# A two-layer hybrid encoder trunk: later key and query transposes, the last channel sum on VectorE, and two output blocks in one feature loop

## The chip, the cores and the metric

The kernel runs on one core of one Trainium2 chip. The metric is the time of one execution on the device in microseconds. The kernel before was run three times: 2420.48, 2420.87 and 2423.06 us, a median of 2420.87. One further execution was taken with the hardware profiler, and every row below is of that one.

## The reference

Two inputs, a prompt of 256 tokens and a sample of 512, go through the same two layers. They share weights and nothing else. Cut to what is computed:

```python
for l in range(2):
    h = rms_norm(x, g_mix[l])
    q, k, v, u, gl = split(h @ w_in[l])
    q, k = rope(rms_norm(q per head)), rope(rms_norm(k per head))
    a = attention(q, k, v)              # 8 heads, 2 key heads, head size 128
    z = u[:1024] * sigmoid(u[1024:])
    z = depthwise_conv(z, 31 taps)      # each channel by itself
    c = silu(layer_norm(z)) @ w_pw[l]
    ga, gc = split(sigmoid(gl + b_gate[l]))
    x = x + (ga * a + gc * c) @ w_out[l]
    h2 = rms_norm(x, g_ffn[l])
    gate, up = split(h2 @ w_gu[l])
    x = x + (silu(gate) * up) @ w_down[l]
return rms_norm(x, g_final)
```

All is float32 with 1024 features, so eight blocks of 128 features.

## The kernel before

**Layout.** Features lie on the 128 partitions and the 768 tokens of both inputs along the rows. A float32 operand of TensorE is split into a high and a low fp32r part (`hi`/`lo`, `Thi`/`Tlo`), and every product is made in three passes: high by high, low by high, high by low (`PASSES`, `proj_a` and `proj_two` from L485 on). Eight PSUM banks are handed out in turn (`PS`, L192), so a new tile waits until the one eight tiles earlier has been read.

**The order.** The program is emitted by one planner. `Clock` (L54) keeps TensorE's time so far: `mm` (L202) and `turn` (L206) add the estimated cost of a matmul and of a transpose. Work that depends on other engines is put down with `clock.at(dt, job)` or `clock.later(dt, job)` and emitted when the planner's clock has passed the due time; `later` also lets a job be called sooner, once. Between these, `tap` (L764) fills VectorE with the taps of the depthwise convolution: 31 instructions for each of eight blocks in each layer, on 783 columns. The engines run their queues in the order in which the instructions were emitted.

**Keys and queries.** `rope_body` projects each of six token tiles (`q0p`, `kp`), and `rotate` (L673) turns the pair of heads: ScalarE copies out of PSUM and squares, VectorE multiplies out of PSUM into `q0r` or `kr`, GpSimd does the two remaining products into `q0t` and the addition. For k, `scale_k` (L700) multiplies on ScalarE after a GpSimd rsqrt (L218). `flip` (L706) then transposes both halves on TensorE (`kT`, `q0T`), and ScalarE and VectorE split the result. The flips come due at `K_FLIP` and `Q_FLIP` (used at L731 to L734) after the last projection, and at the latest with the first score that needs them. After q come the gate projections (`gl_0`, `gl_1`) and the convolution's inputs (`ua`, `ug`).

**Scores.** `h0t0s` is the score tile of head 0 and token tile 0; its sum, reciprocal (`h0t0st`) and scale (`h0t0p`) go over VectorE and ScalarE before TensorE transposes it (`h0t0T`).

**Channel norm.** When a block's 31 taps are done, `add` (L775) adds it into `ysum` on GpSimd. After the eighth, `channel_norm` (L1410) comes due: TensorE takes the mean with a matrix of ones (`mean`), VectorE subtracts it from each block (`centre`, L1423), ScalarE squares (`square`, L1424), VectorE adds the squares (`add`, L1430), and TensorE takes the variance (`var`). A sum comes due 1.0 after its square was put down.

**Output.** Attention and the convolution branch are mixed into eight feature blocks, each split by ScalarE (`mThi`) and VectorE (`mTlo`). `out_body` (L993) multiplies by the output weights: eight output blocks, each in two halves of 384 tokens, each half 24 matmuls (eight features, three passes) and an addition into `x` by VectorE. The loop at L1014 makes blocks 0 to 3 one step each and blocks 4 to 7 a step together.

Of the kernel before, what the change touches and what calls it, by code (L numbers as in the profile page):

```python
# [17 lines left out]
ALU = mybir.AluOpType  # L18
# [137 lines left out]
def trunk(tc, x_in, x_tok, w_a, w_qkv, w_pw, w_out, w_gu, w_down, vecs, gqk, rope, y_out):  # L156
# [4 lines left out]
    with ExitStack() as ctx:  # L161
# [333 lines left out]
            yield  # L495
            return ps

        def proj_two(ws, hT, s, names):

            t0, n = SPLITS[s]  # L500
            ps = [PS(name) for name in names]
            for k in range(KC):
                for w, o in zip(ws, ps):
                    for p, (a, b) in enumerate(PASSES):
                        mm(o[:, :n], w[a][:, k * P:(k + 1) * P], hT.cols(k, b, s),
                           k == 0 and p == 0, k == KC - 1 and p == 2)
# [122 lines left out]
        def layer_blocks(l):  # L629
# [127 lines left out]
            def conv(j, z):  # L757
                wcol = lambda k: vcol(l, V_WDW, k * KC + j)

                def first():  # L760
                    y.y[j] = UC(nm(f"y{j}"))
                    vector.tensor_scalar(y.y[j], z[:, :CONV_N], wcol(0), vcol(l, V_BDW, j), op0=ALU.mult, op1=ALU.add)

                def tap(k):  # L764
                    def f():
                        vector.scalar_tensor_tensor(y.y[j], z[:, k:k + CONV_N], wcol(k), y.y[j],
                                                    op0=ALU.mult, op1=ALU.add)
                    return f

                def last():  # L770
                    y.z_live -= 1
                    tap(CK - 1)()
                    clock.at(1.5, add)

                def add():  # L775
                    if y.ysum is None:
                        y.ysum = XP(nm("ysum"))[:, :CONV_N]
                        nc.gpsimd.tensor_copy(y.ysum, y.y[j])
                    else:
                        nc.gpsimd.tensor_tensor(y.ysum, y.ysum, y.y[j], op=ALU.add)  # L780
                    y.convs += 1
                    if y.convs == KC:
                        clock.at(LN_AFTER, lambda: channel_norm(y))

                taps = [tap(k) for k in range(1, CK - 1)] + [last]
                clock.waiting.append([first] + taps)
# [206 lines left out]
            def out_body(*js):  # L993
                def body(ws):
                    if js[0] == 0:
                        for f in y.gates:
                            f()
                        for j in range(KC):
                            y.xs.append(X(nm(f"x{j}"), j))
                            nc.sync.dma_start(y.xs[j], x_in[j] if l == 0 else x_dram[j])  # L1000
                        y.norm2 = ffn_norm()
                    for s, (t0, n) in enumerate(HALVES):
                        for e, j in enumerate(js):
                            ps = yield from proj_a(ws[e], y.mT, s, nm(f"o{j}_{s}"), HALVES)
                            xs = y.xs[j][:, t0:t0 + n]
                            vector.tensor_tensor(xs, ps[:, :n], xs, op=ALU.add)
                            y.norm2.add(j, s)
                            if s == 1:
                                ws.free(e)
                            if (s, j) == (1, KC - 2):  # L1010
                                weights.next = clock.now + SUMS_AT
                return body

            for js in tuple((j,) for j in range(KH)) + (tuple(range(KH, KC)),):  # L1014
                stream.add([(l, f"out:{j}") for j in js], nm(f"wo{js[0]}"), [w_out[l, j] for j in js], out_body(*js))


# [392 lines left out]
        def channel_norm(y):  # L1410
            l, nm, ys = y.l, y.nm, y.y
            chain = clock.chains[2]
            mean, rstd, sqs = [], [], []
            y.normed = Once(lambda: None)

            def means():
# [5 lines left out]

            def centre(j):  # L1423
                def square():  # L1424
                    sq = Z(nm(f"sq{j}"))
                    act(sq[:, :CONV_N], ys[j], AF.Square)
                    sqs.append(sq)
                    clock.at(1.0, add)

                def add():  # L1430
                    if j:
                        a, b = sqs[0][:, :CONV_N], sqs.pop()[:, :CONV_N]
                        vector.tensor_tensor(a, a, b, op=ALU.add)
# [207 lines left out]
SIG_FIRST = 0.3  # L1641
SIG_EACH = 0.65
K_SCALE = 5.0
K_FLIP = 11.6
Q_FLIP = 10.0
LO_POOL = ((1,), (1, 3))
ADD_POOL = (1, 3, 5)
N_ACC = 0.8
# [80 lines left out]
```

## Time and profile before

| | |
|---|---|
| median of three runs | 2420.87 us (2420.48 to 2423.06) |
| the profiled execution | 2419.15 us |
| its span | 2417.4 us |
| mean granted TensorE clock | 0.972 of full speed |
| DVE busy | 1930.8 us (80%) |
| ACT busy | 1135.9 us (47%) |
| POOL busy | 1300.8 us (54%) |

The span is the time from the first instruction to the last; what lies around it is 1.75 us. PE is TensorE's matmuls and transposes, PEld its weight loads, DVE VectorE, ACT ScalarE, POOL GpSimd. A row of the timeline reads: start, duration, engine, line, operation, output<-input, shape, count, and in brackets the idle time of the engine before it with the instruction that ended it. Tile names have lost their numbers: `L_q0r` is q0r of any layer. An instruction's duration can overlap the next one's start on the same engine.

### The profile page before, as it was taken

To read this page: it belongs to the slowest core of one execution; us is meant where nothing else is said; L and a number is where in the kernel's file an instruction comes from. 1 tells how busy PE (TensorE), PEld (TensorE's weight loads), DVE (VectorE), ACT (ScalarE), POOL (GpSimd) and SP (SyncE) were. 2 spreads that over 40 slices of the span, in tenths; PEclk is the share of its full clock that TensorE was granted. 3 is DMA by queue.
4 is the path that set the end of the run, shared out by engine and by line. 5 is a ranking of instruction groups with operands and counts; after the bars stand their busy time and mean duration, and the time that the engine had idled before them with its cause. 6 is when DMAs were issued, how large, how long until landed. Compare 5 with 4: busy or idle time off the path is not lost. (4 is left out here: it accounts for less than half of the span.)

```text
span 2417.4 us, 34958 instructions
## 1 busy us (share of the span) xinstructions
PE 2239.3 (93%) x13276; PEld 2102.1 (87%) x13276; DVE 1930.8 (80%) x2478; ACT 1135.9 (47%) x2281; POOL 1300.8 (54%) x958
## 2 busy tenths in 40 slices
PE   8898999999979999999998899999999799999997
PEld 7778888888979999999987787888889699999997
DVE  5899999755287798797978999996553877887888
ACT  5324554684244444444443255556833444444443
POOL 4943553532266666666668444535322766666664
PEclk9899999999989999999998999999999899999999
DMA  4111111133212343343421111212341134334332
GB/s 166 36 61 64 58 49 60 64 106 135 97 53 97 126 144 110 128 147 109 157 81 51 53 47 59 66 63 73 112 159 53 35 122 140 122 123 140 122 123 88
DMA packets 72425, 229.60 MB, mean 95 GB/s; under 512 B 8128, under 2 KB 15296, under 8 KB 72256
## 3 DMA queue, kind: packets, MB, share of 16 engines
q1 hardware_dynamic: 72256, 227.37, 27.4%
q8 instruction: 104, 1.70, 0.3%
q14 instruction: 65, 0.53, 0.1%
HBM read 208.46 MB, written 18.87 MB: 94 GB/s over the span
## 5 line engine op out<-in xcount | busy, mean ns | idle before, releaser
L133 DVE SCALAR_TENSOR_TENSOR L_y<-L_z,vec,L_y 128x783 f32<-128x783 f32 x480 | 625.9, 1338 | 2.5
L214 POOL TENSOR_TENSOR wq_L_wgu_0m<-T_L_wgu,wq_L_wgu_0m 128x512 fp32r<-128x512 f32 x168 | 228.4, 1375 | 173.4 <-ACT wq_L_wgu_0m L211 173.4
L211 ACT ACTIVATE wq_L_wgu_0m<-T_L_wgu 128x512 fp32r<-128x512 f32 x168 | 102.6, 630 | 258.5 <-DVE T_L_wgu L133 209.3
L214 POOL TENSOR_TENSOR wq_L_wgu_0m<-st_L_wgu,wq_L_wgu_0m 128x512 fp32r<-128x512 f32 x126 | 179.5, 1426 | 43.3 <-ACT wq_L_wgu_0m L211 43.3
L214 POOL TENSOR_TENSOR lo_L_wgl<-st_L_wgl,hi_L_wgl 128x1024 fp32r<-128x1024 f32 x32 | 101.5, 3178 | 147.9 <-ACT hi_L_wgl L211 121.1
L203 PE MATMUL L_gl<-L_h1h,hi_L_wgl 128*128 128x512 f32 (+1 forms) x512 | 177.7, 347 | 0.6 <-DVE L_h1t4m L133 0.6
L203 PE MATMUL L_gl<-L_h1h,lo_L_wgl 128*128 128x512 f32 (+1 forms) x512 | 174.4, 341 | 0.0
L203 PE MATMUL L_gl<-L_h1l,hi_L_wgl 128*128 128x512 f32 (+1 forms) x512 | 174.0, 340 | 0.0
L214 POOL TENSOR_TENSOR lo_L_wqkv<-st_L_wqkv,hi_L_wqkv 128x1024 fp32r<-128x1024 f32 x24 | 65.4, 2724 | 129.1 <-ACT hi_L_wqkv L211 118.2
L214 POOL TENSOR_TENSOR lo_L_wu<-st_L_wu,hi_L_wu 128x1024 fp32r<-128x1024 f32 (+1 forms) x32 | 82.9, 2594 | 50.4 <-ACT hi_L_wu L211 50.4
L214 POOL TENSOR_TENSOR lo_L_wo<-st_L_wo,hi_L_wo 128x1024 fp32r<-128x1024 f32 x16 | 39.5, 2468 | 127.2 <-ACT hi_L_wo L211 127.2
L203 PEld LDWEIGHTS L_gl<-L_h1h,lo_L_wgl 128*128 128x128 f32 x512 | 97.6, 191 | 11.2
L203 PEld LDWEIGHTS L_gl<-L_h1h,hi_L_wgl 128*128 128x128 f32 x512 | 97.9, 191 | 10.3 <-DVE L_h1t4m L133 0.9
L203 PEld LDWEIGHTS L_gl<-L_h1l,hi_L_wgl 128*128 128x128 f32 x512 | 97.9, 191 | 9.7
L203 PE MATMUL L_o<-L_mThi,hi_L_wo 128*128 128x384 f32 x256 | 88.5, 346 | 6.8 <-ACT L_mThi L211 6.8
L214 POOL TENSOR_TENSOR lo_L_wpw<-st_L_wpw,hi_L_wpw 128x1024 fp32r<-128x1024 f32 x16 | 40.0, 2503 | 100.0 <-ACT hi_L_wpw L211 95.2
L133 DVE TENSOR_TENSOR L_dl<-L_silu,L_dh 128x384 fp32r<-128x384 f32 x80 | 59.5, 782 | 41.1 <-ACT L_dh L211 41.1
L203 PE MATMUL L_c<-L_zsh,hi_L_wpw 128*128 128x256 f32 (+1 forms) x256 | 90.2, 352 | 0.0
L203 PE MATMUL L_ua<-L_h1h,hi_L_wu 128*128 128x256 f32 (+1 forms) x256 | 90.0, 352 | 0.0
L203 PE MATMUL L_ug<-L_h1h,lo_L_wu 128*128 128x256 f32 (+1 forms) x256 | 87.4, 342 | 2.7 <-DVE lo_L_wu L133 2.7
L211 ACT ACTIVATE wq_L_wgu_0m<-st_L_wgu 128x512 fp32r<-128x512 f32 x126 | 78.5, 623 | 22.8 <-POOL wq_L_wgu_0m L214 19.4
L203 PE MATMUL L_ua<-L_h1h,lo_L_wu 128*128 128x256 f32 (+1 forms) x256 | 89.0, 348 | 0.1
(1629 smaller groups left out, 7918.6 us busy)
## 6 DMA issues: line engine op xcount, KB each, us to landing
st_L_wgu<-w_gu SPq DMA_DIRECT2D x88, 512.0 KB, 3.5
st_L_wu<-w_a SPq DMA_DIRECT2D x32, 512.0 KB, 3.5
st_L_wgl<-w_a SPq DMA_DIRECT2D x32, 512.0 KB, 3.5
st_L_wqkv<-w_qkv SPq DMA_DIRECT2D x24, 512.0 KB, 3.5
st_L_wpw<-w_pw SPq DMA_DIRECT2D x16, 512.0 KB, 3.7
st_L_wo<-w_out SPq DMA_DIRECT2D x16, 512.0 KB, 3.7
g_dram<-L_sgl SPq DMA_DIRECT2D x16, 384.0 KB, 2.4
L_gj<-g_dram SPq DMA_DIRECT2D x16, 384.0 KB, 4.3
```

Source lines behind the costliest of these rows:

```text
L133: return f(out, *args, **kw)
L203: nc.tensor.matmul(out, lhsT, rhs, start=start, stop=stop)
L211: nc.scalar.activation(out, in_, func, **kw)
L214: engine.tensor_tensor(lo, x, hi.bitcast(F32), op=ALU.subtract)
```

## The change

`K_FLIP` goes from 11.6 to 21.0 and `Q_FLIP` from 10.0 to 13.0. The eighth addition into `ysum` is issued on VectorE instead of GpSimd. The sums of squares keep their due times, but when a square is put down, sums are issued early until at most one is left waiting. Output blocks 0 and 1 become one step; their first halves go through `proj_two`, which gets a parameter for the token halves, and their second halves follow one after the other.

```diff
--- before.py
+++ after.py
@@ -495,9 +495,9 @@
             yield
             return ps
 
-        def proj_two(ws, hT, s, names):
-
-            t0, n = SPLITS[s]
+        def proj_two(ws, hT, s, names, parts=SPLITS):
+
+            t0, n = parts[s]
             ps = [PS(name) for name in names]
             for k in range(KC):
                 for w, o in zip(ws, ps):
@@ -777,7 +777,8 @@
                         y.ysum = XP(nm("ysum"))[:, :CONV_N]
                         nc.gpsimd.tensor_copy(y.ysum, y.y[j])
                     else:
-                        nc.gpsimd.tensor_tensor(y.ysum, y.ysum, y.y[j], op=ALU.add)
+                        engine = vector if y.convs == KC - 1 else nc.gpsimd
+                        engine.tensor_tensor(y.ysum, y.ysum, y.y[j], op=ALU.add)
                     y.convs += 1
                     if y.convs == KC:
                         clock.at(LN_AFTER, lambda: channel_norm(y))
@@ -1000,8 +1001,11 @@
                             nc.sync.dma_start(y.xs[j], x_in[j] if l == 0 else x_dram[j])
                         y.norm2 = ffn_norm()
                     for s, (t0, n) in enumerate(HALVES):
+                        two = None
+                        if js[0] == 0 and s == 0:
+                            two = yield from proj_two([ws[e] for e in range(2)], y.mT, s, [nm(f"o{j}_{s}") for j in js], HALVES)
                         for e, j in enumerate(js):
-                            ps = yield from proj_a(ws[e], y.mT, s, nm(f"o{j}_{s}"), HALVES)
+                            ps = two[e] if two else (yield from proj_a(ws[e], y.mT, s, nm(f"o{j}_{s}"), HALVES))
                             xs = y.xs[j][:, t0:t0 + n]
                             vector.tensor_tensor(xs, ps[:, :n], xs, op=ALU.add)
                             y.norm2.add(j, s)
@@ -1011,7 +1015,7 @@
                                 weights.next = clock.now + SUMS_AT
                 return body
 
-            for js in tuple((j,) for j in range(KH)) + (tuple(range(KH, KC)),):
+            for js in ((0, 1), (2,), (3,), tuple(range(KH, KC))):
                 stream.add([(l, f"out:{j}") for j in js], nm(f"wo{js[0]}"), [w_out[l, j] for j in js], out_body(*js))
 
 
@@ -1410,7 +1414,7 @@
         def channel_norm(y):
             l, nm, ys = y.l, y.nm, y.y
             chain = clock.chains[2]
-            mean, rstd, sqs = [], [], []
+            mean, rstd, sqs, adds = [], [], [], []
             y.normed = Once(lambda: None)
 
             def means():
@@ -1422,10 +1426,12 @@
 
             def centre(j):
                 def square():
+                    while len(adds) > 1:
+                        adds.pop(0)()
                     sq = Z(nm(f"sq{j}"))
                     act(sq[:, :CONV_N], ys[j], AF.Square)
                     sqs.append(sq)
-                    clock.at(1.0, add)
+                    adds.append(clock.later(1.0, add))
 
                 def add():
                     if j:
@@ -1641,8 +1647,8 @@
 SIG_FIRST = 0.3
 SIG_EACH = 0.65
 K_SCALE = 5.0
-K_FLIP = 11.6
-Q_FLIP = 10.0
+K_FLIP = 21.0
+Q_FLIP = 13.0
 LO_POOL = ((1,), (1, 3))
 ADD_POOL = (1, 3, 5)
 N_ACC = 0.8
```

TensorE, first layer, before: the last projections of q0 around the key transposes; `kT0` and `kT1` are the two key heads, in two banks each.

```order
L203 MATMUL L0_q0p4_969<-hi_L0_wqkv2_1_625,L0_h1l1_351 128x256
L203 MATMUL L0_q0p4_969<-lo_L0_wqkv2_1_626,L0_h1h1_350 128x256
L207 MATMUL L0_kT0_0_999<-ident_137,L0_kr0_569 128x128 x3
L207 MATMUL L0_kT0_1_1003<-ident_137,L0_kr1_570 128x128 x3
L207 MATMUL L0_kT1_0_1013<-ident_137,L0_kr0_569 128x128 x3
L207 MATMUL L0_kT1_1_1017<-ident_137,L0_kr1_570 128x128 x3
L203 MATMUL L0_q0p5_1031<-hi_L0_wqkv2_0_563,L0_h1h1_350 128x256
L203 MATMUL L0_q0p5_1031<-hi_L0_wqkv2_0_563,L0_h1l1_351 128x256
```

After: the same transposes stand between gate matmuls.

```order
L203 MATMUL L0_gl0_1_1081<-L0_h1l1_351,hi_L0_wgl0_0_795 128x512
L203 MATMUL L0_gl0_1_1081<-L0_h1h1_350,lo_L0_wgl0_0_796 128x512
L207 MATMUL L0_kT0_0_1110<-ident_137,L0_kr0_569 128x128 x3
L207 MATMUL L0_kT0_1_1114<-ident_137,L0_kr1_570 128x128 x3
L207 MATMUL L0_kT1_0_1124<-ident_137,L0_kr0_569 128x128 x3
L207 MATMUL L0_kT1_1_1128<-ident_137,L0_kr1_570 128x128 x3
L203 MATMUL L0_gl0_1_1081<-L0_h1h1_350,hi_L0_wgl0_0_795 128x512
L203 MATMUL L0_gl0_1_1081<-L0_h1l1_351,hi_L0_wgl0_0_795 128x512
```

The remaining q0 projections, `gl0_0` and the first 18 matmuls of `gl0_1` have come ahead of the twelve transposes.

TensorE, first layer, before: the channel mean, between two groups of the last q projection `q3p5`.

```order
L203 MATMUL L0_q3p5_4312<-hi_L0_wqkv5_0_3763,L0_h1l1_351 128x256
L203 MATMUL L0_q3p5_4312<-lo_L0_wqkv5_0_3764,L0_h1h1_350 128x256
L203 MATMUL L0_mean0_4329<-L0_ysum_1286,ones_142 128x256
L203 MATMUL L0_mean1_4331<-L0_ysum_1286,ones_142 128x512
L203 MATMUL L0_h4t5s_4335<-L0_kThi1_1011,L0_q2Thi0_3481 128x512
L203 MATMUL L0_h4t5s_4335<-L0_kThi1_1011,L0_q2Tlo0_3482 128x512
L203 MATMUL L0_h4t5s_4335<-L0_kTlo1_1012,L0_q2Thi0_3481 128x512
L203 MATMUL L0_q3p5_4312<-hi_L0_wqkv5_1_3867,L0_h1h1_350 128x256
```

After: the channel mean inside a gate projection.

```order
L203 MATMUL L0_gl5_0_4359<-L0_h1h0_183,hi_L0_wgl5_0_3958 128x256
L203 MATMUL L0_gl5_0_4359<-L0_h1l0_184,hi_L0_wgl5_0_3958 128x256
L203 MATMUL L0_gl5_0_4359<-L0_h1h0_183,lo_L0_wgl5_0_3959 128x256
L203 MATMUL L0_mean0_4377<-L0_ysum_1312,ones_142 128x256
L203 MATMUL L0_mean1_4379<-L0_ysum_1312,ones_142 128x512
L203 MATMUL L0_gl5_0_4359<-L0_h1h0_183,hi_L0_wgl5_0_3958 128x256
L203 MATMUL L0_gl5_0_4359<-L0_h1l0_184,hi_L0_wgl5_0_3958 128x256
```

The score matmuls `h4t5s`, the end of `q3p5` and half of `gl5_0` now stand before the mean instead of behind it.

VectorE, first layer, before: from the last taps of block `y7` to the first subtraction of the mean.

```order
L133 TENSOR_TENSOR L0_h4t2pTlo_4163<-L0_h4t2T_4164,L0_h4t2pThi_4162 128x4x128
L133 SCALAR_TENSOR_TENSOR L0_y7_3708<-L0_z7_3353,vec_114,L0_y7_3708 128x783 x2
L133 TENSOR_REDUCE L0_h4t4st_4213<-L0_h4t4s_4209 128x1
L133 TENSOR_TENSOR L0_q3r0_4071<-L0_q3p2_4178,L0_tab0_445 128x256
L133 TENSOR_TENSOR L0_h4t0m_4224<-L0_h4t0av_4217,L0_sgl4_3871 128x256
L133 TENSOR_TENSOR L0_q3r1_4072<-L0_q3p3_4231,L0_tab0_445 128x256
L133 RECIPROCAL L0_h4t4st_4213<-L0_h4t4st_4213 128x1
L133 TENSOR_TENSOR L0_q3r1_4072<-L0_q3p4_4270,L0_tab0_445 128x256
L133 TENSOR_TENSOR L0_h4t2pTlo_4163<-L0_h4t3T_4286,L0_h4t2pThi_4162 128x4x128
L133 TENSOR_TENSOR L0_y0_504<-L0_y0_504,L0_mean0_4329 128x256
```

After: the same stretch of VectorE.

```order
L133 TENSOR_TENSOR L0_q3r0_4070<-L0_q3p2_4177,L0_tab0_445 128x256
L133 TENSOR_TENSOR L0_h4t0m_4223<-L0_h4t0av_4216,L0_sgl4_3869 128x256
L133 SCALAR_TENSOR_TENSOR L0_y7_3675<-L0_z7_3352,vec_114,L0_y7_3675 128x783
L133 TENSOR_TENSOR L0_q3r1_4071<-L0_q3p3_4230,L0_tab0_445 128x256
L133 RECIPROCAL L0_h4t4st_4212<-L0_h4t4st_4212 128x1
L133 TENSOR_TENSOR L0_ysum_1312<-L0_ysum_1312,L0_y7_3675 128x783
L133 TENSOR_TENSOR L0_q3r1_4071<-L0_q3p4_4269,L0_tab0_445 128x256
L133 TENSOR_TENSOR L0_h4t2pTlo_4162<-L0_h4t3T_4285,L0_h4t2pThi_4161 128x4x128
L133 TENSOR_REDUCE L0_h4t5st_4333<-L0_h4t5s_4329 128x1
```

The addition into `ysum` stands three rows behind the block's last tap; the first subtraction of the mean comes later, behind the reduction of `h4t5s`.

TensorE, first layer, before: the start of the output projection; `o0_0` is block 0, first half.

```order
L203 MATMUL L0_o0_0_5889<-L0_mThi0_5112,hi_L0_wo0_0_5557 128x384
L203 MATMUL L0_o0_0_5889<-L0_mTlo0_5113,hi_L0_wo0_0_5557 128x384
L203 MATMUL L0_o0_0_5889<-L0_mThi0_5112,lo_L0_wo0_0_5558 128x384
L203 MATMUL L0_o0_0_5889<-L0_mThi1_5202,hi_L0_wo0_0_5557 128x384
L203 MATMUL L0_o0_0_5889<-L0_mTlo1_5203,hi_L0_wo0_0_5557 128x384
L203 MATMUL L0_o0_0_5889<-L0_mThi1_5202,lo_L0_wo0_0_5558 128x384
L203 MATMUL L0_o0_0_5889<-L0_mThi2_5332,hi_L0_wo0_0_5557 128x384
```

After: `o1_0` is block 1, first half.

```order
L203 MATMUL L0_o0_0_5889<-L0_mThi0_5112,hi_L0_wo0_0_5557 128x384
L203 MATMUL L0_o0_0_5889<-L0_mTlo0_5113,hi_L0_wo0_0_5557 128x384
L203 MATMUL L0_o0_0_5889<-L0_mThi0_5112,lo_L0_wo0_0_5558 128x384
L203 MATMUL L0_o1_0_5890<-L0_mThi0_5112,hi_L0_wo0_1_5672 128x384
L203 MATMUL L0_o1_0_5890<-L0_mTlo0_5113,hi_L0_wo0_1_5672 128x384
L203 MATMUL L0_o1_0_5890<-L0_mThi0_5112,lo_L0_wo0_1_5673 128x384
L203 MATMUL L0_o0_0_5889<-L0_mThi1_5202,hi_L0_wo0_0_5557 128x384
L203 MATMUL L0_o0_0_5889<-L0_mTlo1_5203,hi_L0_wo0_0_5557 128x384
L203 MATMUL L0_o0_0_5889<-L0_mThi1_5202,lo_L0_wo0_0_5558 128x384
L203 MATMUL L0_o1_0_5890<-L0_mThi1_5202,hi_L0_wo0_1_5672 128x384
```

Each feature is now used for both blocks before the next one is.

## Rows read from the trace of the kernel before

**Rows 1.** Page, busy time of each engine in the whole span.

```profile
PE 2239.3 (93%) x13276; PEld 2102.1 (87%) x13276; DVE 1930.8 (80%) x2478; ACT 1135.9 (47%) x2281; POOL 1300.8 (54%) x958
```

**Rows 2.** TensorE's waits: what waited, releaser, us in total, times, longest.

```profile
PE L_kT L207 <- ACT L_kr L211: 16.0, 6, 7.7
...
PE L_mean L203 <- POOL L_ysum L780: 10.0, 2, 5.1
...
PE L_o L203 <- ACT L_mThi L211: 6.8, 2, 3.5
```

**Rows 3.** Windows: stretch, length, busy time by engine, PEclk, DMA share, GB/s.

```profile
88.89:99.13 10.24, 5.76 (x22) 4.44 (x23) 3.05 (x5) 6.78 (x28) 9.88 (x10) 0.50 0.15 51
96.08:445.62 349.54, 321.38 (x2039) 289.25 (x2038) 339.26 (x377) 169.49 (x374) 175.59 (x122) 0.97 0.18 59
447.29:454.12 6.83, 4.85 (x11) 3.36 (x12) 3.72 (x9) 4.51 (x16) 5.04 (x8) 0.50 0.06 19
1645.37:1648.78 3.41, 3.41 (x7) 2.01 (x8) 2.06 (x5) 1.05 (x5) 2.90 (x6) 0.50 0.00 0
```

**Rows 4.** Timeline of TensorE at the key transposes and the first score transpose.

```profile
92.62 0.47 PE L207 MATMUL L_kT<-ident,L_kr 128*128 128x128 f32 x1 [7.71 <-ACT L_kr L211]
...
182.71 0.69 PE L207 MATMUL L_h0t0T<-ident,L_h0t0p 128*128 128x128 f32 x2 [6.32 <-ACT L_h0t0p L211]
```

**Rows 5.** Timeline of ScalarE: the scaling of k and of the first score.

```profile
92.16 3.62 ACT L211 ACTIVATE L_kr<-L_kr,L_kr 128x128 f32<-128x128 f32 x12 [16.31 <-POOL L_kr L218]
...
182.15 0.51 ACT L211 ACTIVATE L_h0t0p<-L_h0t0p,L_h0t0st 128x256 f32<-128x256 f32 x1 [0.37 <-DVE L_h0t0st L133]
```

**Rows 6.** Timeline of VectorE at the output blocks of both layers.

```profile
610.77 0.69 DVE L133 TENSOR_TENSOR L_mTlo<-L_mj,L_mThi 128x512 fp32r<-128x512 f32 x1 [0.70 <-ACT L_mThi L211]
...
621.93 0.56 DVE L133 TENSOR_TENSOR L_x<-L_o,L_x 128x384 f32<-128x384 f32 x1 [3.64 <-PE L_o L203]
...
626.13 0.56 DVE L133 TENSOR_TENSOR L_x<-L_o,L_x 128x384 f32<-128x384 f32 x1 [3.64 <-PE L_o L203]
...
1822.84 0.56 DVE L133 TENSOR_TENSOR L_x<-L_o,L_x 128x384 f32<-128x384 f32 x1 [3.66 <-PE L_o L203]
```

**Rows 7.** Timeline of VectorE at the q0 projections.

```profile
96.08 0.42 DVE L133 TENSOR_TENSOR L_q0r<-L_q0p,L_tab 128x256 f32<-128x256 f32 x1 [7.72 <-ACT L_q0t L211]
...
101.10 0.41 DVE L133 TENSOR_TENSOR L_q0r<-L_q0p,L_tab 128x256 f32<-128x256 f32 x1
```

**Rows 8.** Timeline of GpSimd behind the q0 projections.

```profile
107.80 3.14 POOL L214 TENSOR_TENSOR lo_L_wu<-st_L_wu,hi_L_wu 128x1024 fp32r<-128x1024 f32 x1
...
113.31 1.33 POOL L694 TENSOR_TENSOR L_q0r<-L_q0r,L_q0t 128x256 f32<-128x256 f32 x1
```

**Rows 9.** Timeline of GpSimd: the last channel sum, first layer.

```profile
447.38 1.84 POOL L780 TENSOR_TENSOR L_ysum<-L_ysum,L_y 128x783 f32<-128x783 f32 x1
```

**Rows 10.** Timeline of TensorE: the channel mean, first layer.

```profile
449.27 2.93 PE L203 MATMUL L_mean<-L_ysum,ones 128*128 128x256 f32 x4 [4.87 <-POOL L_ysum L780]
```

**Rows 11.** Timeline of VectorE ahead of the channel mean.

```profile
443.03 2.60 DVE L133 SCALAR_TENSOR_TENSOR L_y<-L_z,vec,L_y 128x783 f32<-128x783 f32 x2
445.55 0.68 DVE L133 TENSOR_REDUCE L_h4t4st<-L_h4t4s 128x1 f32<-128x512 f32 x1
```

**Rows 12.** Tile view of sq: durations in ns, min/median/max, first and last start.

```profile
L133 DVE TENSOR_TENSOR L_sq<-L_sq,L_sq x14: 965/976/3046, 458.3 to 1673.6; 128x783 f32<-128x783 f32 x14
```

**Rows 13.** Timeline of TensorE: the first output matmul of each layer.

```profile
603.64 0.33 PE L203 MATMUL L_o<-L_mThi,hi_L_wo 128*128 128x384 f32 x1
...
1798.97 0.34 PE L203 MATMUL L_o<-L_mThi,hi_L_wo 128*128 128x384 f32 x1
```

**Rows 14.** Timeline of GpSimd: the weight split of output block 1.

```profile
583.61 2.41 POOL L214 TENSOR_TENSOR lo_L_wo<-st_L_wo,hi_L_wo 128x1024 fp32r<-128x1024 f32 x1 [8.95 <-ACT hi_L_wo L211]
```

**Rows 15.** Page, costliest groups: count, busy us, mean ns of one, idle before.

```profile
L133 DVE SCALAR_TENSOR_TENSOR L_y<-L_z,vec,L_y 128x783 f32<-128x783 f32 x480 | 625.9, 1338 | 2.5
```

**Rows 16.** Tile view of y: the same taps, min/median/max in ns.

```profile
L133 DVE SCALAR_TENSOR_TENSOR L_y<-L_z,vec,L_y x480: 1003/1027/3181, 49.3 to 1640.2; 128x783 f32<-128x783 f32 x160
```

## The prediction, made before the changed kernel was run

> **What bounds the kernel now.** I read the busy times first, then TensorE's waits by what released them, then the stretches around each edited place, and last the single rows there. TensorE (PE) is busy 2239.3 of the span's 2417.4 us [rows 1], so a gain has to come from its idle time or from time that it spends at half clock. The waits that the edits touch are those of the key transposes (kT: 16.0 us in 6 waits, the longest 7.7), of the channel norm's mean (10.0 us in 2) and of the first output block (o: 6.8 us in 2) [rows 2]. The long ones of kT and of the mean are followed by a stretch in which the granted clock is 0.50, the lower of TensorE's two levels, against 0.97 over the long stretch behind it [rows 3]. A wait thus costs its own length and then half of what TensorE does in that stretch.
>
> Not every such microsecond is worth one. From 96.08 to 445.62 us VectorE (DVE) is busy 339.26 of 349.54 us and TensorE 321.38 [rows 3]: there VectorE paces the stage, and what TensorE gains before it is lost where it next waits for VectorE. At the mean and at the output blocks TensorE paces what follows.
>
> **Key and query transposes (K_FLIP, Q_FLIP).** Before, TensorE stops at 84.91 and starts the transposes at 92.62, released by ScalarE's scaling of k, which itself waited 16.31 us for GpSimd's rsqrt [rows 4, 5]. After, 24 matmuls of 256 columns for q, 24 for gl_0 and 18 of 512 for gl_1 stand ahead of them. At 0.175 us for one of 384 columns (24 output matmuls lie between the sums at 621.93 and 626.13: 4.20 us [rows 6]), in proportion 0.117 for 256 and 0.233 for 512, they fill 2.8 + 2.8 + 4.2 = 9.8 us: TensorE comes to the transposes at 94.7, when ScalarE's twelve scalings, from 92.16 to 95.78 [rows 5], are nearly done. The old wait goes. But the q groups moved ahead take PSUM banks in turn, and the transposes then need the banks that VectorE's four q0r products must read first. These come one by one, the first at 96.08 + 0.42, the last at 101.10 + 0.41 = 101.5 [rows 7]: VectorE waits 7.72 us for a ScalarE copy behind those same scalings, which the edit does not move, and has two taps between any two products. From 94.7 to 101.5 are 6.8 us; with the transposes in between I count 5.7 us of new waits against the 7.7 removed. With the half clock that may go (5.76 us busy at 0.50, so 2.9 [rows 3]) TensorE is 5 to 6 us ahead there. GpSimd follows with a weight split of 3.14 us at 107.80 and the last q0r at 113.31 [rows 8], for which the query transposes wait; Q_FLIP moves these too, and about 2 us are left at the next weights. All of it ends at the first score transposes: they wait 6.32 us for a ScalarE scale at 182.15 that VectorE's sum releases [rows 4, 5], and the same taps stand ahead of that sum on VectorE. So I take **0** for both layers, with 0 to +6 us a layer as bounds (a loss would need bank waits beyond 7.7 + 2.9, and the banks give at most 6.8): the cover is that wait of 6.32 us, and if VectorE were faster there the gain would show.
>
> **The last channel sum on VectorE, the order of the square sums.** Before, TensorE waits 4.87 us at the mean until 449.27, that is from 444.40, for a GpSimd addition of 1.84 us at 447.38, behind GpSimd's rope work [rows 9, 10]. After, three score matmuls of 512 columns, 12 of q3p and 12 of gl_0 of 256 come ahead of the mean: 0.7 + 1.4 + 1.4 = 3.5 us, so TensorE arrives at 447.9. VectorE does, from 443.03, two taps (2.60), a reduction (0.68) [rows 11], three products near 0.42 and a reciprocal, which with overlaps of about 0.08 ends at 447.3; then the addition. It waits for nothing but GpSimd's seventh addition, a block earlier, so nothing behind it on VectorE is held up by more than its own length. The trace has none of this kind on VectorE; the nearest is the square sum, two inputs of 128x783 from SBUF: 965 ns at the shortest, 976 in the middle, 3046 at the longest [rows 12]. From 0.97 to 3.05, I take 1.5, since nothing of GpSimd's is certain to stand beside it. The mean is ready at 448.8 and TensorE waits 0.9 us (0.3 to 2.4). Gain: 4.87 of wait, 2.42 of half clock (4.85 busy at 0.50 [rows 3]), less 0.9, is 6.4 us. In the second layer the wait is 5.1 [rows 2], the half-clock stretch holds 3.41 us [rows 3], so 5.1 + 1.7 - 0.9 = 5.9. Sum 12.3. From it go 1.7, an even chance in each layer that the short new wait still ends in a half-clock stretch of 3.4 us, and 1.0 for the variance behind it: its eight squares (ScalarE) and seven sums (VectorE) end by my schedule when TensorE arrives, 0 to 2 us late, 0.5 a layer. The `adds` list adds no instruction: still seven sums, the first behind four subtractions of the mean instead of three, so that its square is further on when VectorE comes to it. That leaves **9.6 us**.
>
> The Trainium skill ("SBUF — State Buffer", section "SBUF: two separate sides") says that VectorE and GpSimd share a port pair as an exclusive lock, taken for a whole instruction by a VectorE operation with two SBUF inputs against a GpSimd operation that reads SBUF. The spread from 965 to 3046 ns of the square sums agrees with that [rows 12]. By it the new addition costs 0.97 or about 3, never the 1.5 that I took: with a free port in both layers my forecast would be 2398.6, with a locked one 2402.8.
>
> **Two output blocks in one feature loop.** Before, the first output block begins at 603.64 [rows 13], and 21 of its 24 matmuls (7 features, 3.7 us) are done by 607.3; the eighth feature's high part comes just before 610.77 and its low part 0.69 later [rows 6]: the wait of 3.3 us, 3.5 in the other layer [rows 2]. After, the second block's first half stands beside it, 42 matmuls or 7.35 us for seven features: TensorE reaches the eighth at 611.0 and waits about 0.35 for the low part at 611.46. Its weights are split by 583.61 + 2.41 = 586.0 [rows 14], ahead of their earlier use. Both blocks are 96 matmuls, 16.8 us, in either order. Before, the fourth sum into x begins at 626.13; after, at 603.64 + 16.8 + 0.1 + 0.35 = 620.9, so 5.2 us. (Of the 22.5 us before, matmuls and wait explain 20.1; the rest I put down to half clock behind the wait, as at the mean.) Second layer: 1822.84 [rows 6] against 1798.97 [rows 13] + 16.8 + 0.1 + 0.5 = 1816.4, so 6.4. Sum **11.6 us**, from 9 (the low part 1.3 us later in both layers) to 12.6 (no wait at all). The first sum into x comes 0.1 us earlier or later, and blocks 2 to 7 are bound by TensorE: nothing waits for what moved.
>
> **Sum.** 0 + 9.6 + 11.6 = 21.2 us. The profiled execution took 2419.15 us, 1.75 over its span, and becomes 2398.0; it lies 1.7 below the median of 2420.87, from which the change gives 2399.7. I predict **2400 us**, own range 2394 to 2405 (new addition free or locked, transposes a little above 0).
>
> **Rivals.**
> - *The mean's gain is given back in the channel norm.* The mean comes earlier, but VectorE's work between it and the variance does not shrink: seven sums at 0.98 are 6.8 us, and three of them that become 3.05 [rows 12] take 6.2 us, which is the gain of a layer. For it: GpSimd's moved rope work now falls beside them. Against: ScalarE's and VectorE's shares in that stretch are 4.51 and 3.72 of 6.83 us [rows 3], so they have room. Only the output term stays: 2420.87 - 11.6 = 2409.
> - *TensorE paces the first stage after all.* Then kT's 16.0 [rows 2] counts as well: 2399.7 - 16.0 = 2384. For it: TensorE is busy 321 of 349 us there. Against: VectorE 339, and the new bank waits.
> - *The waits come back under other names* and the change does not do what it says: TensorE stops as long at the banks, at the variance, at the last feature. 2421, no change. Against: at the output blocks both times follow from counts of matmuls alone.
> - *Slower: VectorE's taps are held up more by GpSimd.* The 480 taps take 1338 ns in the mean [rows 15] and 1027 in the middle [rows 16], 149 us over. Moving the q and k work changes which GpSimd instruction lies beside which tap through the whole stage that VectorE paces. A quarter more is 37 us, less 21: 2437. It decides from 21 us on, which is 44 ns more a tap. Against: the same GpSimd instructions are there, only in another place.
>
> The lock named above from the Trainium skill ("SBUF — State Buffer", "SBUF: two separate sides") is what would make that last rival; taps at 1003 and at 3181 ns agree with it [rows 16], and no row tells how many meet in the new order.
>
> **How the numbers follow.** Forecast 0.58; given back in the channel norm 0.18; first stage paced by TensorE 0.08; no change 0.09; slower 0.07. Within 0.2% (2416 to 2425.7, about what a measurement of this kernel can tell from no change) is the fourth alone; faster is 0.58 + 0.18 + 0.08 = 0.84; slower 0.07. The range runs from 2386, close to the second rival, to 2412, which takes in the first rival; about 0.2 is left out.
>
> **What would show it.** At the mean, a TensorE wait of 0.3 to 2.4 us released by VectorE, and a ysum addition on VectorE of 1 to 3 us. At the output blocks, a wait under 1 us and the fourth sum into x 17.3 us after the first matmul. kT waits released by VectorE's q0r instead of ScalarE, and a longer wait at the first score transposes, by as much as TensorE is ahead: if that wait keeps its 6.3 us while it starts earlier, VectorE was not the pace and I am wrong by up to 16 us. A mean tap above 1.38 us would make me wrong on the other side.

## The result and the profile after

The changed kernel took 2403.61 us (2401.79 to 2405.50, four runs) against 2421.97 us of the kernel before, measured with it: a ratio of 0.9933, 95% interval 0.9921 to 0.9944. Measured again beside the later experiments it gave 0.9936 (0.9924 to 0.9949). So it is 13.6 to 19 us faster. 2400 was forecast, with a range from 2386 to 2412.

TensorE's waits in the kernel after, in the columns of [rows 2]:

```profile
PE L_h0t0T L207 <- ACT L_h0t0p L211: 19.8, 2, 10.7
PE L_h3t3T L207 <- ACT L_h3t3p L211: 11.1, 2, 5.5
PE L_kT L207 <- DVE L_q0r L133: 10.5, 6, 2.0
PE L_h1t3T L207 <- ACT L_h1t3p L211: 6.4, 2, 3.2
...
PE L_mean L203 <- DVE L_ysum L133: 3.2, 2, 1.6
...
PE L_o L203 <- DVE L_mTlo L133: 0.6, 2, 0.3
```

The three waits of [rows 2] have shrunk or changed their releaser: kT waits for VectorE's q0r, the mean for VectorE's sum, the output only for the last low part. In their place stand longer waits for score scales (h0t0T, h3t3T, h1t3T). Of these, the kernel before had the first two, and none at h1t3T:

```profile
PE L_h0t0T L207 <- ACT L_h0t0p L211: 12.5, 2, 6.3
...
PE L_h3t3T L207 <- ACT L_h3t3p L211: 4.5, 2, 2.3
```

To see what is left of the gain one has to compare places. TensorE in the kernel after, at the key transposes, at the first scores of head 0 and head 4, at the mean, and at a late score of head 5; first layer, then second:

```profile
96.36 0.33 PE L207 MATMUL L_kT<-ident,L_kr 128*128 128x128 f32 x1 [1.47 <-DVE L_q0r L133]
...
98.78 0.33 PE L207 MATMUL L_kT<-ident,L_kr 128*128 128x128 f32 x1 [1.87 <-DVE L_q0r L133]
...
101.33 0.47 PE L207 MATMUL L_kT<-ident,L_kr 128*128 128x128 f32 x1 [2.01 <-DVE L_q0r L133]
...
183.04 0.48 PE L207 MATMUL L_h0t0T<-ident,L_h0t0p 128*128 128x128 f32 x1 [9.11 <-ACT L_h0t0p L211]
...
416.23 0.27 PE L207 MATMUL L_h4t0T<-ident,L_h4t0p 128*128 128x128 f32 x1
...
452.30 0.48 PE L203 MATMUL L_mean<-L_ysum,ones 128*128 128x256 f32 x1 [1.59 <-DVE L_ysum L133]
...
509.72 0.47 PE L207 MATMUL L_h5t4T<-ident,L_h5t4p 128*128 128x128 f32 x1 [2.94 <-ACT L_h5t4p L211]
...
601.26 0.33 PE L203 MATMUL L_o<-L_mThi,hi_L_wo 128*128 128x384 f32 x1
...
1257.97 0.28 PE L203 MATMUL L_q0p<-hi_L_wqkv,L_h1h 128*128 128x256 f32 x1
...
1370.58 0.47 PE L207 MATMUL L_h0t0T<-ident,L_h0t0p 128*128 128x128 f32 x1 [10.65 <-ACT L_h0t0p L211]
...
1603.97 0.27 PE L207 MATMUL L_h4t0T<-ident,L_h4t0p 128*128 128x128 f32 x1
...
1697.18 0.46 PE L207 MATMUL L_h5t4T<-ident,L_h5t4p 128*128 128x128 f32 x1 [2.94 <-ACT L_h5t4p L211]
...
1788.87 0.34 PE L203 MATMUL L_o<-L_mThi,hi_L_wo 128*128 128x384 f32 x1
```

TensorE in the kernel before, the places that [rows 4, 13] do not show:

```profile
413.94 0.33 PE L207 MATMUL L_h4t0T<-ident,L_h4t0p 128*128 128x128 f32 x1 [0.40 <-ACT L_h4t0p L211]
...
512.13 0.48 PE L207 MATMUL L_h5t4T<-ident,L_h5t4p 128*128 128x128 f32 x1 [2.92 <-ACT L_h5t4p L211]
...
1266.39 0.28 PE L203 MATMUL L_q0p<-hi_L_wqkv,L_h1h 128*128 128x256 f32 x1
...
1378.37 0.47 PE L207 MATMUL L_h0t0T<-ident,L_h0t0p 128*128 128x128 f32 x1 [6.16 <-ACT L_h0t0p L211]
...
1609.61 0.33 PE L207 MATMUL L_h4t0T<-ident,L_h4t0p 128*128 128x128 f32 x1 [0.42 <-ACT L_h4t0p L211]
...
1707.38 0.47 PE L207 MATMUL L_h5t4T<-ident,L_h5t4p 128*128 128x128 f32 x1 [2.95 <-ACT L_h5t4p L211]
```

Read as differences: at h0t0T the kernel after is 0.33 us late, at h4t0T 2.29 late, at h5t4T 2.41 early, at the first output matmul 2.38 early. In the second layer the stretch from the first q0 matmul to h4t0T takes 346.0 us instead of 343.2, and from h4t0T to h5t4T 93.2 instead of 97.8. So the stage of the taps has become slower, the stage of the channel norm faster. The last rows are VectorE's, in the kernel after: its sum into ysum, and the fourth sum into x of each layer.

```profile
451.01 1.23 DVE L133 TENSOR_TENSOR L_ysum<-L_ysum,L_y 128x783 f32<-128x783 f32 x1
...
618.89 0.56 DVE L133 TENSOR_TENSOR L_x<-L_o,L_x 128x384 f32<-128x384 f32 x1 [3.65 <-PE L_o L203]
...
1806.49 0.56 DVE L133 TENSOR_TENSOR L_x<-L_o,L_x 128x384 f32<-128x384 f32 x1 [3.63 <-PE L_o L203]
```

From the first output matmul the sums into x come after 17.63 and 17.62 us; before it was 22.49 and 23.87 [rows 6, 13]. The span went from 2417.4 to 2400.0 us. Of the 17.4, by the first two rows of the table below, the taps cost 5.3, the norm gave 9.3 and the output 11.3; the other 2.1 lie elsewhere, mostly in the feed-forward part, which the change does not touch. Why they came is not shown.

**Where the taps lost.** VectorE's busy time on the tiles y alone, from h0t4T to h1t3T in the first layer (stretch, length, DVE busy, instructions, then the other engines): before, and after.

```profile
222.66:271.70 49.04, 40.56 (x31) 0.00 (x0) 4.36 (x2) 0.97 0.13 39
```

```profile
222.60:273.77 51.17, 43.86 (x32) 0.00 (x0) 3.85 (x2) 0.93 0.14 44
```

The stretch is 2.13 us longer. VectorE works 3.3 us longer on these tiles in it, with one instruction more, which takes about 1.03 us when nothing holds it up [rows 16]. At its end, VectorE in the kernel after (two single taps):

```profile
266.62 2.53 DVE L133 SCALAR_TENSOR_TENSOR L_y<-L_z,vec,L_y 128x783 f32<-128x783 f32 x1
...
269.19 3.03 DVE L133 SCALAR_TENSOR_TENSOR L_y<-L_z,vec,L_y 128x783 f32<-128x783 f32 x1
```

and GpSimd beside them:

```profile
266.37 1.96 POOL L781 TENSOR_TENSOR L_ysum<-L_ysum,L_y 128x783 f32<-128x783 f32 x1
...
268.29 3.11 POOL L214 TENSOR_TENSOR lo_L_wu<-st_L_wu,hi_L_wu 128x1024 fp32r<-128x1024 f32 x1
```

Each tap ends 0.8 us after the GpSimd instruction beside it has ended (268.33 and 271.40). In the kernel before, VectorE's four taps at the same place, with the third of them by itself, and GpSimd beside them:

```profile
265.30 4.63 DVE L133 SCALAR_TENSOR_TENSOR L_y<-L_z,vec,L_y 128x783 f32<-128x783 f32 x4
...
267.82 1.03 DVE L133 SCALAR_TENSOR_TENSOR L_y<-L_z,vec,L_y 128x783 f32<-128x783 f32 x1
```

```profile
266.87 3.07 POOL L218 TENSOR_TENSOR L_q1r<-L_q1ss,nhalf 128x12 f32<-128x12 f32 x1
```

There a GpSimd power of 12 columns lay beside the last three taps. It took as long as the weight split, and these three taps 1.03 us each; the first of the four, beside other GpSimd work, took 1.42.

Over all 480 taps the mean went from 1338 ns [rows 15] to 1363 (below), which is 12.8 us in sum. But other work of VectorE was held up less: the first of each block's 31 instructions (TENSOR_SCALAR) and the products z of 256 columns. Before, and after (busy us, mean ns, then the idle time ahead of them):

```profile
L133 DVE TENSOR_SCALAR L_y<-L_z,vec 128x783 f32<-128x783 f32 x16 | 25.7, 1609 | 0.4
...
L133 DVE TENSOR_TENSOR L_z<-L_z,L_sg 128x256 f32<-128x256 f32 x16 | 14.5, 904 | 22.8 <-ACT L_sg L211 22.8
```

```profile
L133 DVE TENSOR_SCALAR L_y<-L_z,vec 128x783 f32<-128x783 f32 x16 | 22.7, 1420 | 0.4
...
L133 DVE TENSOR_TENSOR L_z<-L_z,L_sg 128x256 f32<-128x256 f32 x16 | 11.1, 695 | 25.1 <-ACT L_sg L211 25.1
```

The products z also wait 2.3 us longer for ScalarE's sigmoid: a new wait of 1.1 us in each layer. Each engine's busy time in the whole stage of the taps, from the first q0 matmul to h4t0T in both layers, before and after (the first figure is the stage's length):

```profile
sum 686.65, PE 614.95 PEld 551.57 DVE 656.19 ACT 317.91 POOL 375.65; mean PE 307.48 PEld 275.78 DVE 328.09 ACT 158.95 POOL 187.83
```

```profile
sum 691.98, PE 619.21 PEld 557.08 DVE 659.30 ACT 317.49 POOL 364.85; mean PE 309.60 PEld 278.54 DVE 329.65 ACT 158.75 POOL 182.42
```

So of the 5.3 us by which the stage grew, 3.1 are longer work of VectorE and 2.2 are idle time of VectorE.

### The profile page after: what moved, and what is told of

Read it like the earlier page. It is cut to its first block, busy times and chain, and to the rows that moved or that the text cites. A ratio compares the mean times of both kernels' runs of the same rounds, so it can differ in the third digit from the quotient of the medians.

```text
span 2400.0 us, 34938 instructions
## 1 busy us (share of the span) xinstructions
PE 2235.7 (93%) x13276; PEld 2101.9 (88%) x13276; DVE 1933.2 (81%) x2480; ACT 1134.3 (47%) x2281; POOL 1285.0 (54%) x956
## 5 line engine op out<-in xcount | busy, mean ns | idle before, releaser
L133 DVE SCALAR_TENSOR_TENSOR L_y<-L_z,vec,L_y 128x783 f32<-128x783 f32 x480 | 638.7, 1363 | 2.5
L214 POOL TENSOR_TENSOR lo_L_wgl<-st_L_wgl,hi_L_wgl 128x1024 fp32r<-128x1024 f32 x32 | 87.8, 2745 | 147.1 <-ACT hi_L_wgl L211 116.5
L203 PEld LDWEIGHTS L_gl<-L_h1h,lo_L_wgl 128*128 128x128 f32 x512 | 99.0, 193 | 11.6
L203 PE MATMUL L_ug<-L_h1h,hi_L_wu 128*128 128x256 f32 (+1 forms) x256 | 89.8, 351 | 0.0
```

The lines of the kernel that those rows point to most:

```text
L133: return f(out, *args, **kw)
L203: nc.tensor.matmul(out, lhsT, rhs, start=start, stop=stop)
L214: engine.tensor_tensor(lo, x, hi.bitcast(F32), op=ALU.subtract)
```

## The experiments

Each ratio is against the kernel before, run on the same chip. The last three columns are worked out from the starts of TensorE's instructions in each trace, in us, summed over both layers: from the first q0 matmul to h4t0T (the stage of the taps), from h4t0T to h5t4T (mean, variance), and from the first output matmul to the variance behind it.

| kernel | median us | before us | ratio (95%) | taps | norm | output |
|---|---|---|---|---|---|---|
| before | | | 1 | 686.7 | 196.0 | 119.6 |
| changed, first time | 2403.61 | 2421.97 | 0.9933 (0.9921 to 0.9944) | 692.0 | 186.7 | 108.3 |
| e2_out | 2407.20 | 2419.08 | 0.9953 (0.9940 to 0.9967) | 686.6 | 197.3 | 108.5 |
| e3_norm | 2414.28 | 2419.08 | 0.9981 (0.9972 to 0.9989) | 686.8 | 191.5 | 118.3 |
| e4_no_flips | 2401.66 | 2419.08 | 0.9929 (0.9917 to 0.9942) | 687.6 | 190.5 | 108.6 |
| e5_flips_sums | 2417.10 | 2416.31 | 1.0002 (0.9993 to 1.0011) | 691.6 | 192.5 | 118.0 |
| e6_q_only | 2422.81 | 2416.31 | 1.0028 (1.0018 to 1.0037) | 690.8 | 209.5 | 108.3 |
| e7_k_only | 2405.10 | 2416.31 | 0.9952 (0.9940 to 0.9965) | 687.1 | 196.2 | 107.7 |
| e8_ln_later | 2407.14 | 2416.31 | 0.9961 (0.9948 to 0.9973) | 686.8 | 196.9 | 108.2 |
| after_again | 2402.06 | 2417.93 | 0.9936 (0.9924 to 0.9949) | 692.0 | 186.6 | 107.7 |
| e9_q3_ln | 2398.83 | 2417.93 | 0.9922 (0.9909 to 0.9936) | 686.6 | 188.0 | 108.1 |
| e10_gp_twice | 2405.01 | 2417.93 | 0.9948 (0.9936 to 0.9961) | 694.0 | 187.4 | 107.7 |
| e13_gp_none | 2387.47 | 2417.93 | 0.9873 (0.9858 to 0.9888) | 678.6 | 184.9 | 107.7 |

**e2_out: the shared feature loop alone.** On the kernel before, with `proj_two` as in the change:

```diff
+                        if js[0] == 0 and s == 0:
+                            two = yield from proj_two([ws[e] for e in range(2)], y.mT, s, [nm(f"o{j}_{s}") for j in js], HALVES)
...
+            for js in ((0, 1), (2,), (3,), tuple(range(KH, KC))):
```

> The kernel before with output blocks 0 and 1 in one feature loop alone. Theory: the output term is worth what it was worth in the changed kernel, 4.8 us in the first layer and 6.6 in the second, so -11.4, about 2410.5; TensorE's wait at the eighth feature falls from 3.3 us to 0.3. Rival: part of that gain needs the earlier arrival that the norm's edit gives; then -8 or less, 2414.

0.0047 of 2419 are 11.4 us, as the theory had it, and the output stretch is as short as in the changed kernel. TensorE's wait there reads as in the changed kernel: for mTlo, 0.6 us in two waits.

**e3_norm: the sums alone.**

```diff
+                        engine = vector if y.convs == KC - 1 else nc.gpsimd
+                        engine.tensor_tensor(y.ysum, y.ysum, y.y[j], op=ALU.add)
...
+                    while len(adds) > 1:
+                        adds.pop(0)()
```

> The kernel before with the last channel sum on VectorE and the early square sums alone. Theory: the mean's edit is worth what TensorE won between h4t0T and h5t0T in the changed kernel, 4.6 us a layer, so -9.2, about 2412.7. Rival: it is the edit that slowed VectorE ahead of the mean as well; then -4, about 2418, and the tap means ahead of h1t3T and h3t3T are those of the changed kernel (1.349 and 1.359 us).

4.6 us, half of what the theory had. The rival has the size right and the reason wrong: the stage of the taps is as before, and the norm gives 4.5 us instead of 9.3. TensorE still waits at the mean, since its place in the queue is the old one:

```profile
PE L_mean L203 <- DVE L_ysum L133: 6.3, 2, 3.2
```

So half of the norm's gain in the changed kernel needs the flips. The two parts of this edit, the sum on VectorE and the early square sums, were not run apart; the mean's wait alone is 3.7 us shorter than before (6.3 instead of 10.0 [rows 2]).

**e4_no_flips: all but the flips.**

```diff
-K_FLIP = 21.0
-Q_FLIP = 13.0
+K_FLIP = 11.6
+Q_FLIP = 10.0
```

> The changed kernel with K_FLIP and Q_FLIP back at 11.6 and 10.0. Theory (the flips cost 5 us, the parts add up): 2403.6 - 5 = 2398.5, faster than both kernels, and the taps ahead of h1t3T and h3t3T back at 1.27 and 1.20 us. Rival 1 (flips worth 0): 2403.6. Rival 2 (flips worth their 16 us of TensorE's wait): 2416 or more.

The ratio is within the interval of the changed kernel, so the theory's 5 us did not come: the flips are worth nothing in sum, as the first rival had it. But that is two effects: the taps are 4.4 us faster without them, the norm 3.8 us slower.

**e5_flips_sums: the flips without the sum on VectorE and without the output loop.**

```diff
+K_FLIP = 21.0
+Q_FLIP = 13.0
...
+                    adds.append(clock.later(1.0, add))
```

> The kernel before with K_FLIP 21.0, Q_FLIP 13.0 and the early square sums, the last channel sum still on GpSimd and the output blocks apart. Theory: the taps cost 2.5 us a layer, the mean's later place takes 3.5 us of the wait of 4.9 and most of the half clock behind it, some 4.7 a layer: -4.4, about 2414.7 where before has 2419.1. Rival (the prediction's account: flips worth 0, all of the mean's gain is VectorE's addition): 2419. Rival 2 (flips cost 5 and give nothing): 2424.

No change, within 0.1%, as the first rival had it, but not for its reason. The taps lose 4.9 us, the norm gives 3.5: the mean's place is worth something with the GpSimd sum too, but that sum is late as well, and TensorE waits 3.3 us for it.

**e6_q_only and e7_k_only: one flip each in the changed kernel.** For e6 the first of these, for e7 the second:

```diff
-K_FLIP = 21.0
+K_FLIP = 11.6
```

```diff
-Q_FLIP = 13.0
+Q_FLIP = 10.0
```

> The changed kernel with K_FLIP back at 11.6, Q_FLIP still 13.0. Theory: nothing is left of either effect, the time is that of the kernel without flips, 2401.7 where before has 2419.1, and the tap means are 1.27 and 1.20. Rival: Q_FLIP slows the taps, 5 us more, 2406.7.

> The changed kernel with Q_FLIP back at 10.0, K_FLIP still 21.0. Theory: K_FLIP alone moves the mean's place and the taps ahead of h1t3T and h3t3T (means 1.349 and 1.359 us), so the time of the changed kernel: ratio 0.993 to before, about 2403 where before has 2419. Rival: the slower taps come from Q_FLIP; then the taps are back at 1.27 and 1.20 and the time is that of e8, 2397.

Both theories fell, and neither rival had the time. The rivals had the taps better: Q_FLIP alone costs the stage 4.1 us, K_FLIP alone 0.4, which is 1.5 lost in the first layer and 1.1 won in the second. Q_FLIP alone makes VectorE 6.6 us longer busy there and 2.4 less idle, K_FLIP alone 2.0 less busy and 2.5 more idle. But Q_FLIP alone makes the kernel slower than the one before, since the norm takes 13.5 us more. With the mean in its old place and the last pair's transposes later, the variance stands ahead of h5t0T in TensorE's queue and waits for its sums:

```profile
480.33 0.37 PE L203 MATMUL L_var<-ones,L_sq 128*128 128x2 f32 x1 [4.12 <-DVE L_sq L133]
```

And K_FLIP alone gains nothing at the norm (196.2). The flips act on the norm as a pair.

**e8_ln_later: the mean's place without the flips.**

```diff
-LN_AFTER = 5.2
+LN_AFTER = 8.7
```

> The changed kernel with K_FLIP and Q_FLIP back at 11.6 and 10.0, and LN_AFTER 8.7 instead of 5.2, so that the channel mean stands behind the same 3.5 us of matmuls as in the changed kernel while the key transposes stand where they stood before. Theory: what the changed kernel won at the mean (4.6 us a layer from h4t0T to h5t0T) is half the addition on VectorE (2.1 to 2.4 us without the flips) and half the mean's later place; the flips themselves only cost. So -4.7 against the kernel without flips: 2397 where that one had 2401.7 and before 2419.1. Rival: the place is worth nothing without the transposes moved: 2401.7.

It fell too: the mean's wait is gone, and the norm is no shorter than before. It is 6.4 us longer than in e4, which differs in the mean's place alone. TensorE waits behind it instead, at two score transposes:

```profile
464.54 0.48 PE L207 MATMUL L_h4t5T<-ident,L_h4t5p 128*128 128x128 f32 x1 [3.54 <-ACT L_h5t0p L211]
...
512.49 0.47 PE L207 MATMUL L_h5t4T<-ident,L_h5t4p 128*128 128x128 f32 x1 [5.07 <-ACT L_h5t4p L211]
```

The first ends when ScalarE has read the next head's scores (h5t0), the second with its own scale. e7 has the same order there, and 2.0 and 5.1 us of the same waits. Both have the last pair's transposes q3T 12 gate matmuls ahead of h4t5T; the changed kernel has them 12 behind it.

**after_again and e9_q3_ln: the changed kernel once more, and the tap stage of before with the norm of after.** The edit of e9 on the changed kernel:

```diff
-K_FLIP = 21.0
-Q_FLIP = 13.0
+K_FLIP = 11.6
+Q_FLIP = 10.0
-                        clock.at(Q_FLIP, fs[0])
+                        clock.at(13.0 if name.endswith("q3") else Q_FLIP, fs[0])
-LN_AFTER = 5.2
+LN_AFTER = 8.7
```

> The changed kernel itself, beside the next three. Theory and rival alike: the ratio of its first measurement, 0.9933 to before.

> The changed kernel with K_FLIP back at 11.6 and Q_FLIP at 10.0 for the first three query pairs, 13.0 for the last alone, and LN_AFTER 8.7: the stage of the taps in the order of before, the channel norm in the order of the changed kernel. Theory: the flips' loss (2.3 and 2.8 us up to h4t0T) and their gain (4.6 us a layer from h4t0T to h5t4T instead of 2.4) lie in different places and can be had apart. So 4.5 us under the kernel without flips: ratio 0.991, 2395 where before has 2417. Rival: the norm's gain comes only because TensorE arrives later from the taps; then 0.993 as without flips, 2400.

The stages come out as expected: taps 686.6 as before, norm 188.0 (93.2 in the second layer, as in the changed kernel; 94.8 in the first). TensorE at the two ends of the second layer's norm:

```profile
1602.21 0.33 PE L207 MATMUL L_h4t0T<-ident,L_h4t0p 128*128 128x128 f32 x1 [0.42 <-ACT L_h4t0p L211]
...
1695.42 0.48 PE L207 MATMUL L_h5t4T<-ident,L_h5t4p 128*128 128x128 f32 x1 [2.95 <-ACT L_h5t4p L211]
```

e9 differs from e8 in the place of q3T alone. The two ratios lie apart (0.9909 to 0.9936 against 0.9948 to 0.9973), and the norm is 8.9 us shorter: with the later mean, that place makes the gain, and K_FLIP is not needed for it.

Of the kernels that compute everything e9 is the fastest of the study: 2398.83 us (2397.15 to 2400.95) against 2402.06 (2400.91 to 2404.24) of the changed kernel on the same chip. The intervals of the two ratios overlap, so 3 us is the likely gain and not a shown one.

**e10_gp_twice and e13_gp_none: does GpSimd hold up the taps?** Only GpSimd's queue differs from the changed kernel's: twelve copies more, or twelve sums less. The second leaves blocks 1 to 6 out of the mean.

```diff
                         engine.tensor_tensor(y.ysum, y.ysum, y.y[j], op=ALU.add)
+                        if engine is nc.gpsimd:
+                            nc.gpsimd.tensor_copy(y.ysum, y.ysum)
```

> The changed kernel with twelve GpSimd instructions more: each of the channel sums that stay on GpSimd is followed by a copy of the sum onto itself (128x783, about 1.58 us as the first copy). TensorE's, VectorE's and ScalarE's queues are word for word the same. Theory: GpSimd instructions that read SBUF hold up VectorE's taps, a split of 3.1 us cost the taps beside it 1.5 and 1.9 us; so about 1.2 us for each copy, +14 us, ratio 0.999, with the mean tap at 1.39 us instead of 1.363. Rival: GpSimd is busy 54% of the time and the copies lie in its idle time: 0 to 2 us, ratio 0.9935, tap mean unchanged.

```diff
-                        engine = vector if y.convs == KC - 1 else nc.gpsimd
-                        engine.tensor_tensor(y.ysum, y.ysum, y.y[j], op=ALU.add)
+                        if y.convs == KC - 1:
+                            vector.tensor_tensor(y.ysum, y.ysum, y.y[j], op=ALU.add)
```

> The changed kernel without those twelve channel sums (blocks 1 to 6 are left out of the sum, so the mean is not the reference's); the other queues are word for word the same. Theory: each took about 2.5 us on GpSimd and held a tap for some 1.4 us: -17 us, ratio 0.986, mean tap 1.33 us. Rival: no change, 0.9933.

The taps (busy us, mean ns) in the changed kernel, with the copies, and without the sums:

```profile
L133 DVE SCALAR_TENSOR_TENSOR L_y<-L_z,vec,L_y 128x783 f32<-128x783 f32 x480 | 638.7, 1363 | 2.5
```

```profile
L133 DVE SCALAR_TENSOR_TENSOR L_y<-L_z,vec,L_y 128x783 f32<-128x783 f32 x480 | 649.9, 1386 | 2.5
```

```profile
L133 DVE SCALAR_TENSOR_TENSOR L_y<-L_z,vec,L_y 128x783 f32<-128x783 f32 x480 | 625.5, 1335 | 2.5
```

The tap means came as the theory said: 11.2 us more for twelve copies (0.93 each), 13.2 less for twelve sums (1.1 each). The time followed in one direction only. Without the sums the stage is 13.4 us shorter and the kernel about 15 us faster (0.9873 against 0.9936). All of it is VectorE's work: 645.9 us of the stage instead of 659.3, with 32.7 idle in both.

```profile
sum 678.61, PE 611.40 PEld 549.56 DVE 645.90 ACT 317.68 POOL 337.17; mean PE 305.70 PEld 274.78 DVE 322.95 ACT 158.84 POOL 168.58
```

With the copies the stage is 2.0 us longer and the kernel about 3 slower, where 14 were expected. The stage of the taps, and the first instruction of each block, with the copies:

```profile
sum 694.02, PE 616.46 PEld 553.77 DVE 663.56 ACT 317.72 POOL 378.69; mean PE 308.23 PEld 276.89 DVE 331.78 ACT 158.86 POOL 189.34
```

```profile
L133 DVE TENSOR_SCALAR L_y<-L_z,vec 128x783 f32<-128x783 f32 x16 | 16.4, 1026 | 0.4
```

Most of the other 9 us is in these rows. Each block's first instruction takes 6.3 us less in sum than in the changed kernel: one at 162.48 there lies beside a weight split and takes 2.77 us, while with the copies a copy of 1.47 us lies beside it and it takes 1.20. And VectorE is 2.2 us less idle in the stage.

## Why the prediction came out right

The forecast was 21.2 us, measured are 13.6 to 19. By the prediction's own steps:

- **Output loop, 11.6 us.** Right: 11.3 in the output stretch, 11.4 by e2 alone. By layer the fourth sum came 4.9 and 6.2 us sooner after the first output matmul (5.2 and 6.4 forecast), and the residual wait is 0.3 us (0.35).
- **Mean, 9.6 us.** The size is right (9.3), and so is the wait: 1.6 us released by VectorE, where 0.9 (0.3 to 2.4) was forecast, and 1.23 us for the addition (1.5). The half clock behind the mean is gone in both layers, where the sum had taken off 1.7 us for an even chance that it stays: the granted clock is 1.00 from 452.30 to 459.00 and from 1639.80 to 1646.00, where it was 0.50 before [rows 3]. But TensorE and VectorE came there some 3 us later than forecast, TensorE at 452.30 - 1.59 = 450.7 instead of 447.9, mostly because the taps before had lost 2.3. And the working hid who earns it: it put the 3.5 us of work ahead of the mean under the addition's heading. By e3 the sums earn 4.5; the rest needs a later place of the mean and of q3T together, which K_FLIP and Q_FLIP set here. The prediction said nothing of q3T, whose place is worth some 9 us (196.9 in e8 against 188.0 in e9). So the size of this term is in part luck.
- **Key and query transposes, 0 us.** Right where the working looked: bank waits of 1.47 + 1.87 + 2.01 = 5.35 us (5.7 forecast), and h0t0T at 183.04 instead of 182.71, with its wait grown from 6.32 to 9.11. This is the step that failed behind that point: its bounds, 0 to +6 us a layer, held no loss, and the stage lost 2.5 to 2.8 us a layer. "The same taps stand ahead of that sum" is true; GpSimd's instructions beside the later taps are others. It was the mechanism of the slower rival, at 25 ns a tap where 44 would have decided; since other instructions were held up less, 3.1 us of it are left, and 2.2 us of new idle time of VectorE come to that. These 5.3 us are more than the forecast is off by the spans (21.2 against 17.4): the 2.1 us won elsewhere, which no term of the sum foresaw, hide a part of them, and that is luck.
- **Rivals.** That the mean's gain is given back in the channel norm did not happen in this kernel; it did in e7 and e8, by waits at two score transposes, not by slower square sums (19.5 us in sum there, 21.2 before). That TensorE paces the first stage is ruled out: kT's wait of 7.7 us fell, and h0t0T came no sooner.

The Trainium skill ("SBUF — State Buffer", "SBUF: two separate sides") has the loser of the shared port wait for the whole instruction of the winner. The taps beside the sum and the split agree, ending 0.8 us after them; those beside the power of 3.07 us do not, at 1.03 us each. In the kernel before, twelve taps lie wholly inside such powers of 12 columns and took 1.02 to 1.04 us. By the measurement, such a power is no blocker for the time that the profile gives it. The new addition took 1.23 us, neither the 0.97 nor the 3 that the prediction read from the lock. It ended 0.8 us after the GpSimd product during which it began, as the taps did:

```profile
450.96 0.44 POOL L692 TENSOR_TENSOR L_q3t<-L_q3t,L_tab 128x128 f32<-128x128 f32 x1
```

What stays open: why, with the later mean, q3T ahead of h4t5T makes TensorE wait there was read from the waits and not taken apart; the kernel before has q3T ahead of h4t5T too, and no wait there. The flips have no time without the early square sums: with the flips alone (e1_flips) the engines' queues block one another for ever (a deadlock).

## What to carry to other kernels

A wait that disappears from a stage paced by another engine buys nothing there, but the moved work still changes which instructions lie beside each other on VectorE and GpSimd, and that has a price of its own: look at the whole stage behind a moved instruction, up to the next place where the pacing engine changes. Where one number sets several places (here a flip's due time for four query pairs and, through the planner's clock, for the mean), cost each place by itself; two that only gain together can lose alone, as Q_FLIP did. Counts of matmuls between two fixed ends were the safest term here: the output loop came within 0.3 us.

## What the runs showed of the hardware

A tap of 128x783 with two SBUF inputs takes 1.03 us by itself [rows 16] (1.00 to 1.04 for the 232 taps of the kernel before that have no GpSimd instruction beside them); beside a GpSimd sum of 1.96 us it took 2.53, beside a GpSimd split of 3.11 us 3.03, and beside a GpSimd power of 12 columns and 3.07 us 1.03. A GpSimd copy of 128x783 cost VectorE 0.93 us of tap time, a sum 1.1; yet the twelve copies made VectorE only 4.3 us longer busy in the stage of the taps, since its other instructions there were held up less.

It seems that GpSimd's instruction can be the one that is held up, too. In the kernel before, one weight split lasted 9.31 us, over a row of seven taps at 0.96 us each; the 24 splits of the q, k and v weights, of the same size, last 2.72 us in the mean.

```profile
149.04 9.31 POOL L214 TENSOR_TENSOR lo_L_wgl<-st_L_wgl,hi_L_wgl 128x1024 fp32r<-128x1024 f32 x1 [7.85 <-ACT hi_L_wgl L211]
```

```profile
148.46 6.70 DVE L133 SCALAR_TENSOR_TENSOR L_y<-L_z,vec,L_y 128x783 f32<-128x783 f32 x7
```
